# Rotary embedding of half the head on one core: three whole tiles loaded first, then stores and the last load in another order

## The chip, the cores and the metric

One core of a Trainium2 chip runs the kernel. The metric is the device time of one execution in microseconds (us). The kernel before takes 161.53 us in the median of 8 runs (161.33 to 161.8).

## The reference

`x` is (16, 512, 16, 64) in float32: batch, position, head, dimension. `cos` and `sin` are (512, 32), of which only the first 16 columns are used. Of each head's 64 numbers the first 32 are rotated as two quarters of 16, and the last 32 are copied:

```
x1, x2 = x[..., :32], x[..., 32:]
rotated_first  = x1[..., :16] * cos[..., :16] - x1[..., 16:] * sin[..., :16]
rotated_second = x1[..., :16] * sin[..., :16] + x1[..., 16:] * cos[..., :16]
out = concatenate([rotated_first, rotated_second, x2], axis=-1)
```

So 33.55 MB are read and 33.55 MB are written, with four elementwise passes over half of the data in between.

## The kernel before

**Tiles.** The 8192 rows of `x` (batch times position, each of 16 x 64 numbers) are cut into T = 4 tiles. A tile has 128 partitions with K = 16 neighbouring rows each, 64 KB to a partition, 8.39 MB in all. `ring` (L45) is one buffer in SBUF with NS = 3 slots; tile t lies in slot t % 3, so tile 3 takes the slot of tile 0 and can be loaded only when tile 0 has been stored. The rotation works in place in the slot, and the store reads from the slot, which carries the copied half along.

**Transfers.** `load` (L54, recorded as L55) and `store` (L57, recorded as L58) move rows lo to hi of each partition of one tile. Both are issued by SyncE (SP), one after the other in the order of the program; an instruction of SP that waits holds up all behind it. Only tile 2's store is issued by GpSimd (POOL), on a queue of its own (q0; SP's is q1). Both queues are worked off by the same 16 DMA engines.

**Tables.** `cos` and `sin` are loaded by POOL (L63, L64), spread over the partitions by a shuffle and copies on VectorE (DVE, L73 to L86), and end up in `table`.

**Rotation.** `rotate(t, lo, hi)` (L90) is four DVE instructions over rows lo to hi of a tile: two multiplications (L96 into `b_t` in PSUM, L97 in place), a subtraction (L98) and an addition (L101). A tile is rotated in two pieces of 8 rows (KC = 8), tile 2 in pieces of 8, 5 and 3 rows (KM = 13).

**Order.** SP issues load(0), load(1), the first half of load(2); then, when tile 0 is rotated, store(0), the second half of load(2) and load(3), which waits for store(0) to land; then store(1), then store(3). DVE rotates the tiles 0, 1, 2, 3 in turn. store(1) would be free to go when tile 1 is rotated; a dependency written by hand (L118) makes it wait for the end of the 5-row piece of tile 2 (`near`, L114). store(2), on POOL, goes when tile 2 is rotated.

Of the kernel before, what the change touches and what calls it, by code (L numbers as in the profile page):

```python
# [1 line left out]

# [4 lines left out]


@with_exitstack
def kernel(  # L10
    ctx: ExitStack,
    tc: tile.TileContext,
    x: bass.AP,
    cos: bass.AP,
    sin: bass.AP,
    out: bass.AP,
):
    nc = tc.nc
    fp32 = mybir.dt.float32
    P = 128  # L20
    B, S, H, D = x.shape
    Q = D // 4
    HF = D // 2

    K = 16
    T = B * S // (P * K)
    PB = S // K
    REP = P // PB  # L30
    R = H * D
    NS = 3
    KC = K // 2
    KM = 13

    xf = x.rearrange("b s h d -> (b s h d)").rearrange("(t p f) -> t p f", t=T, p=P)
    of = out.rearrange("b s h d -> (b s h d)").rearrange("(t p f) -> t p f", t=T, p=P)
    cosf = cos.rearrange("(p k) j -> p (k j)", k=K)
    sinf = sin.rearrange("(p k) j -> p (k j)", k=K)

    const_pool = ctx.enter_context(tc.tile_pool(name="const", bufs=1))
    b_pool = ctx.enter_context(tc.tile_pool(name="bp", bufs=1, space=bass.MemoryType.PSUM))


    ring = const_pool.tile([P, NS, K, H, D], fp32)  # L45
    stage = const_pool.tile([P, 2, K, HF], fp32)
    spun = const_pool.tile([P, 2 * K, Q], fp32)
    packed = const_pool.tile([PB, 2 * K, Q], fp32)
    table = const_pool.tile([P, 2, K, 2, Q], fp32)

    def rows(t, lo, hi):
        return ring[:, t % NS, lo:hi].rearrange("p k h d -> p (k h d)")

    def load(t, lo=0, hi=K):  # L54
        return nc.sync.dma_start(out=rows(t, lo, hi), in_=xf[t, :, lo * R : hi * R])  # L55

    def store(t, lo=0, hi=K, queue=nc.sync):  # L57
        return queue.dma_start(out=of[t, :, lo * R : hi * R], in_=rows(t, lo, hi))  # L58


    nc.vector.memset(stage[:, :, :, 0:Q], 0.0)  # L61
    spread = stage.rearrange("(j b) t k i -> j b t (k i)", b=REP)
    nc.gpsimd.dma_start(out=spread[:, 0, 0], in_=cosf)  # L63
    nc.gpsimd.dma_start(out=spread[:, 0, 1], in_=sinf)  # L64
    load(0)
    load(1)
    load(2, 0, KC)

    PQ = PB // REP
    nc.vector.stream_shuffle(  # L73
        out=spun[:],
        in_=stage.rearrange("p t k j -> p (t k) j")[:, :, 0:Q],
        mask=[j % PQ * REP for j in range(PB)],
    )
    for q in reversed(range(REP)):
        n = PQ * (q + 1)
        nc.vector.tensor_copy(out=packed[0:n], in_=spun[q * PB : q * PB + n])  # L80

    for r in range(REP):
        nc.vector.tensor_copy(  # L83
            out=table[r * PB : (r + 1) * PB].rearrange("p t k c j -> p (t k) c j"),
            in_=packed.unsqueeze(2).to_broadcast((PB, 2 * K, 2, Q)),
        )  # L86
    C = table[:, 0].rearrange("p k c j -> p k (c j)")
    Sn = table[:, 1].rearrange("p k c j -> p k (c j)")

    def rotate(t, lo, hi):  # L90
        x1 = ring[:, t % NS, lo:hi, :, 0:HF]
        c = C[:, lo:hi].unsqueeze(2).to_broadcast((P, hi - lo, H, HF))
        s = Sn[:, lo:hi].unsqueeze(2).to_broadcast((P, hi - lo, H, HF))
        b_full = b_pool.tile([P, KC, H, HF], fp32, name="b_t")
        b_t = b_full[:, 0 : hi - lo]
        nc.vector.tensor_mul(out=b_t, in0=x1, in1=s)  # L96
        nc.vector.tensor_mul(out=x1, in0=x1, in1=c)  # L97
        nc.vector.tensor_sub(  # L98
            out=x1[:, :, :, 0:Q], in0=x1[:, :, :, 0:Q], in1=b_t[:, :, :, Q:HF]
        )  # L100
        return nc.vector.tensor_add(  # L101
            out=x1[:, :, :, Q:HF], in0=x1[:, :, :, Q:HF], in1=b_t[:, :, :, 0:Q]
        )

    rotate(0, 0, KC)
    rotate(0, KC, K)
    store(0)
    load(2, KC, K)
    load(3)
    rotate(1, 0, KC)  # L110
    rotate(1, KC, K)
    behind_loads = store(1)
    rotate(2, 0, KC)
    near = rotate(2, KC, KM)  # L114
    rotate(2, KM, K)
    store(2, queue=nc.gpsimd)

    tc.add_manual_dep(  # L118
        behind_loads.ins,
        near.ins.name,  # L120
        mybir.DependencyInfo(mybir.DependencyClass.Sync, mybir.DependencyReason.DATA),
        reason="the store follows the loads at the DMA engines",
    )
    rotate(3, 0, KC)
    rotate(3, KC, K)
    store(3)


# [1 line left out]
_INS = ['x', 'cos', 'sin']  # L130
_OUTS = [((16, 512, 16, 64), 'float32')]


# [23 lines left out]
```

## Time and profile before

| what | value |
|---|---|
| median of 8 runs | 161.53 us (161.33 to 161.8) |
| the profiled execution | 161.36 us, span 159.4 us |
| DVE busy | 112.9 us (71%), 47 instructions |
| POOL busy | 1.9 us |
| the 16 DMA engines | 67.24 MB, 98% of the span (85.6% for SP's queue, 12.4% for POOL's) |
| one 8-row rotation | 13.44 us; 4.43, 4.42, 2.29 and 2.28 us for its four instructions, the last two overlapping slightly |
| DVE idle ahead of the first rotation | 14.3 us for `sin`, then 1.8 us for tile 0 |

How to read it: the span is the time from the first to the last instruction of the profiled execution; the device time is 2.0 us more. A transfer is seen at three points: its issue, an instruction on SP or POOL; the packets that the 16 engines move for it; and its landing, when all 16 engines have reported the end. The list of DMA issues gives the median time from issue to landing; asked for a stretch that holds one issue alone, it gives the time of that one. What stands in the queue ahead of a transfer is part of that time. Where both queues have work, packets of POOL's and of SP's take turns in this trace.

### The profile page before, as it was taken

How to read it: one execution, taken by the hardware profiler on the slowest of the kernel's cores; microseconds unless marked ns; L12 is line 12 of the kernel's file. 1: busy time of each engine (PE TensorE's matmuls, PEld its weight loads, DVE VectorE, ACT ScalarE, POOL GpSimd, SP SyncE). 2: the span in 40 equal slices, each digit the busy share in tenths (PEclk: the TensorE clock that was granted, in tenths of full speed). 3: DMA queues.
4: the chain of work that ended last, by engine and by line, in shares of the span. 5: the costliest groups of instructions: out<-in, count | busy, mean ns of one | idle time of the engine just before them, and what ended most of it. 6: DMA issues, size and time to landing. Idle time of an engine off the chain costs nothing.

```text
span 159.4 us, 115 instructions
## 1 busy us (share of the span) xinstructions
DVE 112.9 (71%) x47; POOL 1.9 (1%) x7
## 2 busy tenths in 40 slices
DVE  1000959999999999999999999999999990000000
POOL 3000000000000000000000000010000000000000
DMA  7969979799699699699996996996996996998966
GB/s 263 543 263 543 444 345 526 345 444 526 280 493 543 263 526 526 263 395 461 461 526 280 510 526 263 526 526 263 526 526 263 526 493 296 526 428 362 526 263 263
DMA packets 1360, 67.24 MB, mean 422 GB/s; under 512 B 176, under 2 KB 176, under 8 KB 208
## 3 DMA queue, kind: packets, MB, share of 16 engines
q1 hardware_dynamic: 1152, 58.72, 85.6%
q0 software_dynamic: 208, 8.52, 12.4%
HBM read 33.69 MB, written 33.55 MB: 422 GB/s over the span
## 4 chain that ended last, share of the span: by engine, by line
DVE 62%; DMA 14%; issue 5%; DVEq 1%
DVE b_t L96 22%; DVE ring L97 22%; DMA ring<-in_x_dram 14%; DVE ring L101 10%; DVE ring L98 7%; DVEq L152 1%; DVEq L96 0%
## 5 line engine op out<-in xcount | busy, mean ns | idle before, releaser
L96 DVE TENSOR_TENSOR b_t<-ring,table 128x4096 f32<-128x4096 f32 (+2 forms) x9 | 35.6, 3959 | 2.1 <-DMA ring<-in_x_dram 1.8
L97 DVE TENSOR_TENSOR ring<-ring,table 128x4096 f32<-128x4096 f32 (+2 forms) x9 | 35.6, 3951 | 0.3
L98 DVE TENSOR_TENSOR ring<-ring,b_t 128x2048 f32<-128x2048 f32 (+2 forms) x9 | 18.5, 2050 | 0.3
L101 DVE TENSOR_TENSOR ring<-ring,b_t 128x2048 f32<-128x2048 f32 (+2 forms) x9 | 18.4, 2043 | 0.0
L73 DVE LOAD_MASK_SELECT spun<-stage x1 | 0.0, 14 | 14.3 <-DMA stage<-in_sin_dram 14.3
L83 DVE COPY table<-packed 32x1024 f32<-32x1024 f32 x4 | 2.7, 683 | 0.1
L58 POOL DMA_DIRECT2D out_dram<-ring x1 | 0.6, 559 | 101.6 <-DVE ring L101 101.6
L80 DVE COPY packed<-spun 32x512 f32<-32x512 f32 (+3 forms) x4 | 1.7, 416 | 0.1
L61 DVE MEMSET stage<- 128x512 f32 x1 | 0.5, 485 | 0.9 <-PEq L141 0.9
L73 DVE STREAM_SHUFFLE spun<-stage 128x512 f32<-128x512 f32 x1 | 0.7, 723 | 0.0
L63 POOL DMA_DIRECT2D stage<-in_cos_dram x1 | 0.6, 642 | 1.3 <-DVE stage L61 1.3
L64 POOL DMA_DIRECT2D stage<-in_sin_dram x1 | 0.5, 532 | 0.0
L141 POOL MEMSET const-bfloat16-1.0<- 128x1 bf16 x1 | 0.1, 101 | 0.0
L141 POOL MEMSET const-float32-0.0<- 128x1 f32 x1 | 0.1, 98 | 0.2 <-issue 0.2
L141 POOL MEMSET const-float32-1.0<- 128x1 f32 x1 | 0.1, 98 | 0.0
L141 POOL MEMSET const-uint8-127<- 128x1 uint8 x1 | 0.1, 98 | 0.0
## 6 DMA issues: line engine op xcount, KB each, us to landing
ring<-in_x_dram SPq DMA_DIRECT2D x2, 4096.0 KB, 40.7
stage<-in_cos_dram POOLq DMA_DIRECT2D x1, 64.0 KB, 8.9
stage<-in_sin_dram POOLq DMA_DIRECT2D x1, 64.0 KB, 13.2
ring<-in_x_dram SPq DMA_DIRECT2D x3, 29.0
out_dram<-ring SPq DMA_DIRECT2D x3, 27.4
out_dram<-ring POOLq DMA_DIRECT2D x1, 39.5
```

The lines of the kernel that those rows point to most:

```text
L58: return queue.dma_start(out=of[t, :, lo * R : hi * R], in_=rows(t, lo, hi))
L61: nc.vector.memset(stage[:, :, :, 0:Q], 0.0)
L63: nc.gpsimd.dma_start(out=spread[:, 0, 0], in_=cosf)
L64: nc.gpsimd.dma_start(out=spread[:, 0, 1], in_=sinf)
L73: nc.vector.stream_shuffle(out=spun[:], in_=stage.rearrange("p t k j -> p (t k) j")[:, :, 0:Q], mask=[j % PQ * REP for j in range(PB)],)
L80: nc.vector.tensor_copy(out=packed[0:n], in_=spun[q * PB : q * PB + n])
L83: nc.vector.tensor_copy(out=table[r * PB : (r + 1) * PB].rearrange("p t k c j -> p (t k) c j"), in_=packed.unsqueeze(2).to_broadcast((PB, ...
L96: nc.vector.tensor_mul(out=b_t, in0=x1, in1=s)
L97: nc.vector.tensor_mul(out=x1, in0=x1, in1=c)
L98: nc.vector.tensor_sub(out=x1[:, :, :, 0:Q], in0=x1[:, :, :, 0:Q], in1=b_t[:, :, :, Q:HF])
L101: return nc.vector.tensor_add(out=x1[:, :, :, Q:HF], in0=x1[:, :, :, Q:HF], in1=b_t[:, :, :, 0:Q])
L152: with _tile.TileContext(nc) as tc:
```

## The change

The loads in front are three whole tiles. store(0), ready when tile 0 is rotated, waits by hand for the third instruction (the subtraction) of the first piece of tile 1. Tile 1 is rotated in pieces of 7, 7 and 2 rows (KA = 7, KB = 14), tile 2 in two of 8. The first half of store(1) goes when its 14 rows are rotated; then tile 3 is loaded in two halves, ordered behind it on SP without a wait of their own for it. The second half of store(1) waits for the first multiplication of tile 3's first piece, and store(2), still on POOL, for the second one. store(3) is as before. `rotate` now returns its first three instructions.

```
-    load(2, 0, KC)
+    load(2)
...
     rotate(0, 0, KC)
     rotate(0, KC, K)
-    store(0)
-    load(2, KC, K)
-    load(3)
-    rotate(1, 0, KC)
-    rotate(1, KC, K)
-    behind_loads = store(1)
+    head = store(0)
+    behind(head, rotate(1, 0, KA)[2])
+    rotate(1, KA, KB)
+    rotate(1, KB, K)
+
+
+    part = store(1, 0, KC)
+    for lo, hi in ((0, KC), (KC, K)):
+        follow(load(3, lo, hi), part)
     rotate(2, 0, KC)
-    near = rotate(2, KC, KM)
-    rotate(2, KM, K)
-    store(2, queue=nc.gpsimd)
-
-    tc.add_manual_dep(
-        behind_loads.ins,
-        near.ins.name,
-        mybir.DependencyInfo(mybir.DependencyClass.Sync, mybir.DependencyReason.DATA),
-        reason="the store follows the loads at the DMA engines",
-    )
-    rotate(3, 0, KC)
+    rotate(2, KC, K)
+    marks = rotate(3, 0, KC)
+    behind(store(1, KC, K), marks[0])
+    behind(store(2, queue=nc.gpsimd), marks[1])
     rotate(3, KC, K)
     store(3)
```

`behind` is the same dependency by hand as before (a wait on a semaphore), and `follow` one that only fixes the order of issue on an engine:

```
+    def behind(transfer, point, kind=mybir.DependencyClass.Sync):
+        tc.add_manual_dep(
+            transfer.ins,
+            point.ins.name,
+            mybir.DependencyInfo(kind, mybir.DependencyReason.DATA),
+            reason="issue the transfer near the end of the one in front of it",
+        )
+
+    def follow(transfer, other):
+        behind(transfer, other, mybir.DependencyClass.NoSync)
```

More of the change, by code (lines that the diff above doesn't have):

```diff
@@ L33 @@
     KC = K // 2
-    KM = 13
+    KA, KB = 7, 14
     xf = x.rearrange("b s h d -> (b s h d)").rearrange("(t p f) -> t p f", t=T, p=P)
@@ L95, in rotate @@
         b_t = b_full[:, 0 : hi - lo]
-        nc.vector.tensor_mul(out=b_t, in0=x1, in1=s)
-        nc.vector.tensor_mul(out=x1, in0=x1, in1=c)
-        nc.vector.tensor_sub(
+        first = nc.vector.tensor_mul(out=b_t, in0=x1, in1=s)
+        second = nc.vector.tensor_mul(out=x1, in0=x1, in1=c)
+        third = nc.vector.tensor_sub(
             out=x1[:, :, :, 0:Q], in0=x1[:, :, :, 0:Q], in1=b_t[:, :, :, Q:HF]
         )
-        return nc.vector.tensor_add(
+        nc.vector.tensor_add(
             out=x1[:, :, :, Q:HF], in0=x1[:, :, :, Q:HF], in1=b_t[:, :, :, 0:Q]
         )
+        return first, second, third
+    def behind(transfer, point, kind=mybir.DependencyClass.Sync):
[7 more added lines that the diff above has]
+        behind(transfer, other, mybir.DependencyClass.NoSync)
     rotate(0, 0, KC)
     rotate(0, KC, K)
-    store(0)
-    load(2, KC, K)
-    load(3)
-    rotate(1, 0, KC)
-    rotate(1, KC, K)
-    behind_loads = store(1)
-    rotate(2, 0, KC)
-    near = rotate(2, KC, KM)
-    rotate(2, KM, K)
-    store(2, queue=nc.gpsimd)
-    tc.add_manual_dep(
-        behind_loads.ins,
-        near.ins.name,
-        mybir.DependencyInfo(mybir.DependencyClass.Sync, mybir.DependencyReason.DATA),
-        reason="the store follows the loads at the DMA engines",
-    )
-    rotate(3, 0, KC)
+    head = store(0)
[5 more added lines that the diff above has]
+        follow(load(3, lo, hi), part)
+    rotate(2, 0, KC)
+    rotate(2, KC, K)
+    marks = rotate(3, 0, KC)
+    behind(store(1, KC, K), marks[0])
+    behind(store(2, queue=nc.gpsimd), marks[1])
     rotate(3, KC, K)
```

## The prediction

> **What bounds the kernel now.** I read the summary first, then the chain of work that ended last, then the issues of DMAs one at a time, then the order of instructions around the edits.
>
> ```profile
> DVE 112.9 (71%) x47; POOL 1.9 (1%) x7
> ...
> DMA packets 1360, 67.24 MB, mean 422 GB/s; under 512 B 176, under 2 KB 176, under 8 KB 208
> ...
> q1 hardware_dynamic: 1152, 58.72, 85.6%
> q0 software_dynamic: 208, 8.52, 12.4%
> ...
> DVE 62%; DMA 14%; issue 5%; DVEq 1%
> ```
>
> The chain names DVE, because it starts at the last instruction and goes back through the issue of store(3), which waits for DVE. But the two queues keep the 16 DMA engines at 98% of the span. Which of the two decides is read from the time from issue to landing, here of single issues, in stretches that hold one each: store(0) issued at 49.82, load(3) at 71.6, store(1) at 98.80, store(2) at 104.52 and store(3) at 131.1.
>
> ```profile
> out_dram<-ring SPq DMA_DIRECT2D x1, 21.8
> ...
> ring<-in_x_dram SPq DMA_DIRECT2D x1, 29.0
> ...
> out_dram<-ring SPq DMA_DIRECT2D x1, 33.2
> ...
> out_dram<-ring POOLq DMA_DIRECT2D x1, 39.5
> ...
> out_dram<-ring SPq DMA_DIRECT2D x1, 27.4
> ```
>
> Issue plus time gives the landings: store(0) 71.6, load(3) 100.6, store(1) 132.0, store(2) 144.0, store(3) 158.5. By the same sum load(0) lands at 0.74 + 22.1 = 22.8, load(1) at 1.2 + 41.0 = 42.2, the halves of tile 2 at 1.6 + 50.3 = 51.9 and 50.2 + 31.1 = 81.3. A tile behind another takes 19.3 to 19.4 (load(1) after load(0), load(3) after the second half of tile 2). Three stores lie between 100.6 and 158.5: 57.9 = 3 x 19.3. So nothing idles there, and store(3) needs 27.4 instead of 19.3 only because 8 us of older stores stand in front of it. DVE could end several us later and change nothing. The stages by windows say the same (columns: length, DVE and POOL busy, clock, DMA share, GB/s):
>
> ```profile
> 51.30:99.90 48.60, 48.18 (x17) 0.00 (x0) 1.00 1.00 430
> 70.50:99.50 29.00, 28.72 (x12) 0.00 (x0) 1.00 1.00 434
> 99.50:157.50 58.00, 31.34 (x12) 0.56 (x1) 1.00 1.00 434
> ```
>
> The transfers decide, and they already run back to back at 434 GB/s. What is lost after the start is small: store(0) takes 71.6 - 51.9 = 19.7 from the landing in front, **0.4 more** than a tile, where the engines go over from a store to a load. The change moves the same bytes, so it can win at most about this 0.4 and otherwise only lose, by letting the engines run dry.
>
> **The change, step by step.** The end is a sum of landings; each edit is asked whether the next transfer is there in time.
>
> *How early must one be issued?* store(1) was issued at 98.80, 1.8 ahead of the landing of load(3) at 100.6, and the three stores after it lost nothing: a lead of 1.8 is enough. From the other side: load(0), with nothing ahead, lands 22.1 after its issue, 2.8 more than a tile (some of it the table's packets). So the lead needed lies between 0 and 2.8; I take 1.8, the row of a store behind a load, as the nearest.
>
> *Three whole tiles first.* The second half of tile 2 comes forward: load(2) lands at 51.9 + 9.7 = 61.6. DVE reads it only at about 77, so nobody waits for it.
>
> *store(0) held back.* Nothing else on SP is ready, so its wait delays no one. Tile 0's rotation ends at 49.83 as before. The 5-row and the 8-row piece take 90.16 to 98.81 = 8.65 and 76.72 to 90.16 = 13.44, so 1.60 per row and 0.65 on top; 7 rows take 11.84. The subtraction starts after two multiplications of about 3.92 and lasts 2.29 - 0.27 = 2.02: it ends at 59.7. Issue at 59.72 against load(2) at 61.6 is a lead of 1.8, the proven one. Cost 0; at the other bound 1.0.
>
> ```profile
> 97.30 1.48 DVE L101 TENSOR_TENSOR ring<-ring,b_t 128x1280 f32<-128x1280 f32 x1
> 98.80 0.34 SPq L58 DMA_DIRECT2D out_dram<-ring  x1
> ...
> 104.26 4.43 DVE L96 TENSOR_TENSOR b_t<-ring,table 128x4096 f32<-128x4096 f32 x1
> 104.52 0.56 POOL L58 DMA_DIRECT2D out_dram<-ring  x1 [101.65 <-DVE ring L101]
> ```
>
> These rows give the price of a wait by hand: the addition ends at 98.78 and SP issues at 98.80; POOL needs 0.26 after its release.
>
> *First half of store(1), then load(3).* The first two pieces of tile 1 end at 49.83 + 2 x 11.84 = 73.5, and the half store queues on SP then; store(0) is on the engines until 61.6 + 19.3 = 80.9. Load(3), behind it on SP, waits for that landing and is issued at about 81, while the half store covers the engines until 80.9 + 9.7 = 90.6. So the wait of SP is hidden by 9 us of store; without this half in between it would cost up to 2.8. The 0.4 for going from store to load is paid here instead of at 71: half store lands 91.0, the halves of load(3) 100.6 and **110.3**.
>
> *Rotations.* The number of DVE instructions is unchanged (nine pieces), so is the sum: tile 1 gains 0.65 for a third piece, tile 2 loses it. Tile 3's first piece starts at 104.26 as before; its half is there since 100.6. The second piece starts at 117.7, against 110.3.
>
> *Second half of store(1).* It waits for the first multiplication: 104.26 + 4.43 = 108.7. Lead 110.3 - 108.7 = 1.6, **0.2 short** of the proven one; only store(3), not due until 131.1, is behind it on SP. Cost 0 if less lead is needed, 1.2 if 2.8 is. I take 0.1, near the row of 1.8, because an early engine among the 16 waits longer than the late one that sets the landing.
>
> *store(2).* The second multiplication ends at 104.26 + 4.47 + 4.42 = 113.15, POOL issues at 113.4. Before, its first packets appear in a stretch that begins 4.9 after the issue at 104.52, with SP's packets in front; 113.4 + 4.9 = 118.3, while the half store lasts until 110.3 + 9.7 = 120. Hidden. The queue of POOL then works alone until store(3) arrives at 131.1, when about 8 us of store(2) are left, the same cover as before.
>
> *Cut transfers.* Two halves cost 9.7 + 9.7 against 19.3 for a whole: at most 0.1. There are four halves instead of two: 0.05 taken.
>
> *Sum.* 110.3 + 0.1 + 2.5 x 19.3 + 0.05 = 158.7 for the last landing, against 158.5: **+0.15 to 0.2**. On the profiled execution of 161.36 that is 161.5; its time lies 0.17 below the median of the runs, and on the median of 161.53 it is **161.7**.
>
> A rule that speaks against the change: the Trainium skill, "DMA: Bandwidth & Descriptors", section "Rules for kernel authors", wants a DMA issued early, so that its fixed cost is overlapped, and the section "Anatomy of one DMA" puts that cost at about 2.0 us; a lead of 1.8 and one of 1.6 would then lose 0.2 and 0.4, and my estimate by that page is 162.1. The row at 98.80, with 1.8 and no loss, speaks for the lower end, and the sum above uses only the row.
>
> **Rivals.**
>
> *Leads too short (slower), 0.25.* store(0) and the second half of store(1) come too late, and the engines run dry twice. For it: load(0)'s 2.8 with empty queues. Against it: the row at 98.80. It decides from a needed lead of 1.9 (0.1 + 0.3 = 0.4 together). At 2.8 it costs 1.0 + 1.2 = 2.2 and gives 163.7; half way, at 2.3, 0.5 + 0.7 = 1.2 and 162.7.
>
> *The turn gets cheaper (faster), 0.12.* The 0.4 at the turn from store to load falls away, as the stream turns between transfers of half a tile, and the leads suffice: 161.1. Against it: the number of such turns stays at one, and if load(3) landed 0.4 earlier, at 109.9, the lead of the second half would shrink to 1.2.
>
> *POOL's queue alone is slower, 0.05.* From 120 to 131 only store(2) is left for the engines. The trace has no such stretch. If it ran at half of the rate there, 11 us would move 5.5 us of work: 167.
>
> *The change doesn't do what it says, 0.02.* If load(3) came ahead of the half store on SP, the engines would be empty from 80.9 until load(3) starts: up to 2.8, 164.4.
>
> **Chances and range.** Forecast, within 0.2% (0.3 us, about what a measurement of this kernel can tell): 0.56. Faster by more: 0.12. Slower by more: 0.25 + 0.05 + 0.02 = 0.32. Range: down to 161.1 for the cheaper turn, up to 162.8, past the half-way case of the short leads; beyond that lie the full 2.8 and the last two rivals, some 0.17 in all.
>
> **What would show it.** Right: load(2) lands near 61.6, store(0) issues near 59.7 and lands at 80.9 to 81.3, load(3) near 110.3, store(3) near 158.7, DMA share at 1.00 in windows around 61 and 110. Short leads: the landing of store(0) minus that of load(2) well over 19.7, or the last 2.5 tiles taking over 48.4. A slow POOL queue: GB/s under 430 between 120 and 131. A cheaper turn: under 48.7 from the landing of load(2) to that of load(3). I would be wrong at the root if DVE ended last, that is, if store(3) were issued later than 138, when store(2) runs out.

## The result, and the profile after

The changed kernel takes 162.30 us in the median of 11 runs (162.03 to 163.24), the kernel before 161.52 (31 runs). The ratio is **1.0058**, 95% interval 1.0046 to 1.0069: slower by 0.8 us. The profiled execution took 162.25 us with a span of 160.2, against 161.36 and 159.4.

The summary of the changed kernel's page, the lines that answer to those of the prediction:

```profile
DVE 112.9 (70%) x47; POOL 1.9 (1%) x7
...
DMA packets 1504, 67.24 MB, mean 420 GB/s; under 512 B 192, under 2 KB 192, under 8 KB 224
...
DVE 62%; DMA 14%; issue 4%; DVEq 1%
```

VectorE does the same work in the same time, and the bytes are the same. There are more packets, because four transfers are halves instead of two, and the mean rate falls from 422 to 420 GB/s. So the time went at the DMA engines, and the landings say where. Single issues of the changed kernel with their times to landing: store(0), issued at 59.82, the first half of store(1) at 73.6, its second half at 108.80, store(2) at 113.53, store(3) at 131.2:

```profile
out_dram<-ring SPq DMA_DIRECT2D x1, 21.2
...
out_dram<-ring SPq DMA_DIRECT2D x1, 4096.0 KB, 17.7
...
out_dram<-ring SPq DMA_DIRECT2D x1, 4096.0 KB, 16.6
...
out_dram<-ring POOLq DMA_DIRECT2D x1, 31.2
...
out_dram<-ring SPq DMA_DIRECT2D x1, 27.9
```

The halves of load(3), issued at 81.0 and 81.4, needed 20.1 and 29.4; load(2), issued at 1.6, needed 60.0.

| landing, us | predicted | measured |
|---|---|---|
| load(2) | 61.6 | 61.6 |
| store(0) | 80.9 | 81.0 |
| first half of store(1) | 91.0 | 91.3 |
| load(3), first half | 100.6 | 101.1 |
| load(3), second half | 110.3 | 110.8 |
| store(3) | 158.7 | 159.1 |

Up to 81.0 all is as predicted, and from 110.8 to the end 48.3 pass, against 48.4 predicted. In between, where the engines go over from a store to loads, 0.4 more is lost than predicted (29.8 instead of 29.4). The rest is mostly at the end: the span ends 1.1 after the last landing instead of 0.9.

**A measure of the loss.** A turn, below, is the place where the engines go over from loads to a store, or from a store to loads. In a window, GB/s over DMA share is the speed of the packets while they run. Both count whole packets, so the edges of a short window can push the share above or below 1, but not their quotient. The undisturbed value is 434. Share x length x (1 - speed/434) is the time lost to slow packets; idle gaps between packets are not in it and show in the landings. The windows (length, DVE and POOL busy, clock, DMA share, GB/s) of the kernel before at its turn from load to store (46 to 56), its turn from store to load (66 to 76), and late in the stores:

```profile
46.00:56.00 10.00, 9.93 (x4) 0.00 (x0) 1.00 1.03 446
66.00:76.00 10.00, 9.93 (x4) 0.00 (x0) 1.00 0.87 364
...
146.00:156.00 10.00, 0.00 (x0) 0.00 (x0) 1.00 1.00 433
```

and of the changed kernel at its turns from load to store (56 to 66, 105 to 115) and from store to load (85 to 95):

```profile
56.00:66.00 10.00, 9.90 (x5) 0.00 (x0) 1.00 1.12 485
85.00:95.00 10.00, 9.93 (x4) 0.00 (x0) 1.00 1.02 410
105.00:115.00 10.00, 9.93 (x3) 0.56 (x1) 1.00 1.03 446
```

446/1.03 and 485/1.12 are 433: at the turns from load to store no packets are slow, before and after. At the turn from store to load the speed is 364/0.87 = 418 before, a loss of 0.3, and 410/1.02 = 402 after, a loss of **0.75**. The engines do not run dry there, since the packets of the trace follow each other without a gap; they run slower. The slow ones are the last store packet of the engines and some of the first loads: the last 32 KB packet took 1.5 to 2.3 us instead of 1.21; before, the last 64 KB packet took 2.4 to 3.2 instead of 2.42.

### The profile page after: what moved, and what is told of

Read it like the earlier page. It is cut to its first block, busy times and chain, and to the rows that moved or that the text cites. A ratio compares the mean times of both kernels' runs of the same rounds, so it can differ in the third digit from the quotient of the medians.

```text
span 160.2 us, 117 instructions
## 1 busy us (share of the span) xinstructions
DVE 112.9 (70%) x47; POOL 1.9 (1%) x7
## 4 chain that ended last, share of the span: by engine, by line
DVE 62%; DMA 14%; issue 4%; DVEq 1%
DVE b_t L96 22%; DVE ring L97 22%; DMA ring<-in_x_dram 14%; DVE ring L101 10%; DVE ring L98 8%; DVEq L162 1%; DVEq L96 0%
## 6 DMA issues: line engine op xcount, KB each, us to landing
out_dram<-ring POOLq DMA_DIRECT2D x1, 31.2
```

## The experiments

Ratios are to the kernel before on the same chip, from 5 rounds each; the losses come from windows of 10 us by the measure above, in one profiled execution, and are good to about 0.1 (share and rate are rounded). Each kernel turns twice from load to store; one number is that of the first turn, two are those of both.

| kernel | ratio (95%) | load to store | store to load |
|---|---|---|---|
| before | 1 | 0, 0 | 0.3 |
| changed | 1.0058 (1.0046 to 1.0069) | 0, 0 | 0.75 |
| b_s0_halves | 1.0073 (1.0060 to 1.0086) | 0.85 | 0.1 |
| b_s0_tail | 1.0024 (1.0015 to 1.0033) | 0 | 0.5 |
| b_l2_16k | 1.0057 (1.0043 to 1.0071) | 1.0 | 0.05 |
| a_s1_parts | 1.1352 (1.1336 to 1.1367) | - | - |
| a_load_near | 1.0056 (1.0041 to 1.0071) | 0, 0 | 0.85 |
| a_s0_early | 1.0060 (1.0046 to 1.0073) | 1.1, 0 | 0 |
| b_s1_early | 1.0063 (1.0049 to 1.0078) | 0, 1.2 | 0.45 |
| b_load_near | 1.0013 (1.0005 to 1.0022) | 0 | 0.7 |
| b_s0_halves_near | 1.0032 (1.0020 to 1.0044) | 0 | 0.7 |
| b_load_9us | 1.0000 (0.9991 to 1.0009) | 0 | 0.4 |
| a_s1_whole | 1.0054 (1.0040 to 1.0069) | 0, 0.1 | 0.8 |
| b_s0_2_14 | 1.0018 (1.0009 to 1.0027) | 0.2 | 0.3 |

Names with b_ are edits of the kernel before, with a_ of the changed one. The first theory (A) was that the halved store, whose packets are 32 KB, covers less of the start of the loads behind it.

**b_s0_halves**

```
-    store(0)
+    store(0, 0, KC)
+    store(0, KC, K)
```

> The kernel before with store(0) issued as two halves of 8 rows, so that the packets in front of the turn from store to load are 32 KB instead of 64 KB; what follows the turn is unchanged. The turn is measured as the time from the landing of the last load of the first batch to the landing of load(3), less 2.5 tiles of 19.3 us: 0.5 us in the kernel before, 1.0 in the changed one. Theory A (a small store packet in front of the turn covers less of the start of the loads): turn 0.8 to 1.1, time up by 0.3 to 0.6 us, ratio 1.002 to 1.004. Theory B (the size of the load packets behind the turn, or how they are cut, sets the price): turn 0.4 to 0.6, ratio 0.9995 to 1.001. Theory C (the waits by hand, POOL's queue or the end of the stream make the changed kernel slower, the turn only by chance): as B.

Slower by more than A asks, and for another reason. Its windows, at the turn from load to store and at the one from store to load:

```profile
46.00:56.00 10.00, 9.93 (x4) 0.00 (x0) 1.00 1.02 406
68.00:78.00 10.00, 9.93 (x4) 0.00 (x0) 1.00 1.02 439
```

The loss moved to the turn from **load to store** (406/1.02 = 398), and the other turn became all but free (430). Without a wait of its own, the first half of store(0) was issued at 36.45, when its 8 rows were rotated, and stood in the queue for some 13 us ahead of its turn.

**b_s0_tail**

```
-    store(0)
+    store(0, 0, 14)
+    store(0, 14, K)
```

> The kernel before with store(0) cut into 14 and 2 rows, so that the last packets in front of the turn are 8 KB. A: the price of the turn rises beyond that of 32 KB, to 1.0 to 1.5 us, ratio 1.003 to 1.007. B and C: turn 0.4 to 0.6, ratio at most 1.001.

Its window at the turn from store to load:

```profile
66.00:76.00 10.00, 9.93 (x4) 0.00 (x0) 1.00 0.99 406
```

Between the theories: slower by 0.24%, with a loss of 0.5 at the turn (406/0.99 = 410, of which some 0.06 is the greater length of 8 KB packets for their bytes). A, by which 8 KB should cost more than 32 KB, does not fit as a rule of size.

**b_l2_16k**

```
-    load(2, 0, KC)
+    load(2, 0, 12)
...
-    load(2, KC, K)
+    load(2, 12, K)
```

> The kernel before with 12 rows of tile 2 in the first batch and 4 behind the turn: the first load packets behind the turn are 16 KB instead of 32 KB, the store in front is unchanged (64 KB). The first batch is 2.75 tiles, and the turn is measured from its last landing less 2.25 tiles. A: turn 0.4 to 0.6, ratio 0.999 to 1.001. B: turn 0.7 to 1.0, ratio 1.002 to 1.004. C: ratio 0.999 to 1.001.

The ratio is B's, but not the place. The windows at the turn from load to store and from store to load:

```profile
51.00:61.00 10.00, 9.93 (x3) 0.00 (x0) 1.00 0.96 372
72.00:82.00 10.00, 9.90 (x5) 0.00 (x0) 1.00 0.97 419
```

372/0.96 = 388 is a loss of 1.0 at the turn from load to store, where store(0), issued at 50.03, had stood in the queue for about 6 us. The turn to the 16 KB loads is free (419/0.97 = 432), if behind a turn that was paid, so the agreement with B is by chance. B cannot explain the change in any case, since the loads behind the turn are of 32 KB packets in both kernels.

**a_s1_parts**

```
-    part = store(1, 0, KC)
+    def store_part(t, lo, hi):
+        return nc.sync.dma_start(out=of[t, lo:hi, :], in_=ring[lo:hi, t % NS].rearrange("p k h d -> p (k h d)"))
+
+    part = store_part(1, 0, 64)
...
-    behind(store(1, KC, K), marks[0])
+    behind(store_part(1, 64, 128), marks[0])
```

> The changed kernel with tile 1's store halved by partitions (0 to 63, then 64 to 127, all 16 rows) instead of by rows: same bytes in each half, but packets of 64 KB in front of the turn; waits, loads and queues unchanged, the first half goes at 77.4 instead of 73.5, still ahead of the end of store(0). A: turn back to 0.4 to 0.6, 0.4 to 0.6 us faster than the changed kernel, ratio to before 1.000 to 1.003. B and C: turn 0.9 to 1.1, ratio 1.004 to 1.007.

It says nothing on A: a store of 64 partitions ran at half the rate. The window of its first half:

```profile
80.00:100.40 20.40, 20.23 (x7) 0.00 (x0) 1.00 0.99 207
```

The engines are busy for the whole of it, but a 64 KB packet takes 5.1 us instead of 2.42.

After these runs the theories were about how long a transfer of the other direction has been queued: D (it slows the turn in either direction), E (only the first such turn of a run is paid), F (going from store to load costs, whatever the lead).

**a_load_near**

```
-    for lo, hi in ((0, KC), (KC, K)):
-        follow(load(3, lo, hi), part)
-    rotate(2, 0, KC)
+    thirds = [load(3, lo, hi) for lo, hi in ((0, KC), (KC, K))]
+    for transfer in thirds:
+        follow(transfer, part)
+    behind(thirds[0], rotate(2, 0, KC)[2])
```

> The changed kernel with one wait more: the first half of load(3) waits for the subtraction of tile 2's first piece (end near 88.7 us), about 1.2 us ahead of the end of the half store in front, instead of being queued from 81.0. Theory D (a transfer of the other direction that is queued well ahead of the turn slows the last packets in front of it; one issued about 1 us ahead does not): packets in front of the turn back to 1.2 us, 0.6 to 0.8 us faster than the changed kernel, ratio to before 0.998 to 1.001. Theory E (only the first early-queued turn of a run is paid): the same here. Theory F (going from store to load costs this, whatever the lead): unchanged, 1.004 to 1.007, or slower by a gap.

Issued at 88.90, just ahead of the turn, and nothing won: 1.0056. The window at the turn:

```profile
85.00:95.00 10.00, 9.93 (x4) 0.00 (x0) 1.00 1.05 419
```

419/1.05 = 399. D's gain did not come, but half of what D said did. Short windows that hold only the last store packets (from 88.50) and only the first load packets (from 90.00) show it, first in the changed kernel, then in a_load_near:

```profile
88.50:89.50 1.00, 1.00 (x2) 0.00 (x0) 1.00 1.87 524
90.00:91.20 1.20, 1.17 (x2) 0.00 (x0) 1.00 1.10 437
...
88.50:89.50 1.00, 1.00 (x2) 0.00 (x0) 1.00 1.24 524
90.00:91.20 1.20, 1.17 (x2) 0.00 (x0) 1.00 1.59 437
```

With the load queued early the last store packets are slow (524/1.87 = 280) and the first loads less so (437/1.10 = 397). With the load issued late the store packets are normal (423) and the first loads slow (437/1.59 = 275). So the time of issue decided which packets paid, and not how much.

**a_s0_early**

```
     head = store(0)
-    behind(head, rotate(1, 0, KA)[2])
+    rotate(1, 0, KA)
```

> The changed kernel without the wait of store(0): it is queued at 49.9, some 11 us ahead of the turn from load to store near 61, instead of at 59.8. D: that turn now costs 0.8 to 1.0 us too, ratio to before 1.009 to 1.012. E: the first turn is paid and the turn from store to load is free, so about as the changed kernel, 1.004 to 1.007. F: no change at 61, 1.004 to 1.007, the turn from store to load still paid.

Windows at the turns load to store (61), store to load (91), load to store (110):

```profile
54.00:64.00 10.00, 9.93 (x4) 0.00 (x0) 1.00 0.87 328
87.00:97.00 10.00, 9.93 (x4) 0.00 (x0) 1.00 1.00 433
105.00:115.00 10.00, 9.93 (x3) 0.56 (x1) 1.00 0.97 419
```

328/0.87 = 377: store(0), now issued at 49.93, costs 1.1 at its turn, and the turn from store to load costs nothing. The sum hardly moves: 1.0060. E describes this.

**b_s1_early**: the call of `tc.add_manual_dep` for `behind_loads` is left out.

> The kernel before without the wait of store(1), which is then queued at about 76.7, some 23 us ahead of the turn from load to store near 99.8. D: 0.8 to 1.0 us slower, ratio 1.005 to 1.007, the loss in the packets around 97 to 100. E: the turn near 70 is early-queued too and comes first (0.3 us paid as before), so this one is free: 0.999 to 1.001. F: no change, 0.999 to 1.001.

Windows at the turns load to store (51), store to load (71), load to store (100):

```profile
46.00:56.00 10.00, 9.93 (x4) 0.00 (x0) 1.00 1.05 452
66.00:76.00 10.00, 9.93 (x4) 0.00 (x0) 1.00 0.89 367
93.00:103.00 10.00, 9.83 (x7) 0.00 (x0) 1.00 0.86 321
```

The early store costs 1.2 (321/0.86 = 373), although the turn near 71 was paid too. E falls as it was put. What holds in all four kernels with an early store (b_s0_halves, b_l2_16k, a_s0_early, b_s1_early): it costs 0.85 to 1.2. Where a turn from store to load follows (three of them), that one is nearly free.

**b_load_near**: the second half of load(2) waits for a multiplication of tile 1, which is cut 6, 8, 2; store(1) waits for the subtraction of its piece instead of the addition.

```
+    rotate(1, 0, 6)
+    point = rotate(1, 6, 14)[1]
+    rotate(1, 14, K)
...
+    tc.add_manual_dep(
+        rest.ins,
+        point.ins.name,
...
-    near = rotate(2, KC, KM)
+    near = rotate(2, KC, KM)[2]
```

> The kernel before with the second half of load(2) issued at about 69.0 (wait for the second multiplication in a piece of 8 rows of tile 1, now cut 6, 8, 2) instead of at 50.2, so 1.1 to 1.5 us ahead of the end of store(0); the wait of store(1) is moved to the subtraction of the same 5-row piece (98.0 us, since the further piece of tile 1 adds 0.65 on VectorE). D and E: the 0.3 us in the packets at 68 go, 0.2 to 0.5 us faster, ratio 0.997 to 0.999. F: unchanged or slower by a small gap, 1.000 to 1.003.

Its window at the turn:

```profile
66.00:76.00 10.00, 9.90 (x5) 0.00 (x0) 1.00 0.90 360
```

Slower by 0.13%, with 0.7 lost at the turn (360/0.90 = 400): a load issued late, at 69.17, is no help and probably a little worse. Here too the last store packets took their normal 2.42 us and the first loads were slow (1.2 to 2.2 us instead of 1.21). D's gain falls, F stands. That left the size of the price: why 0.3 before and 0.75 after? G blames how long the load had been queued.

**b_s0_halves_near**: store(0) in halves, the first with a wait for the end of tile 0's rotation.

```
...
-    store(0)
...
+    head = store(0, 0, KC)
...
+    store(0, KC, K)
```

> The kernel before with store(0) in two halves again, both issued at 49.8 as the whole was, so that the turn from load to store stays unpaid and only the packets in front of the turn from store to load change, from 64 KB to 32 KB. Theory A (the small store packet in front of the turn): loss at the turn near 70 about 0.8 us instead of 0.3, ratio 1.003 to 1.005. Theory G (the time for which load(3) had been queued: 9 us in the changed kernel, 20 before): 0.3 to 0.45 us, ratio 1.000 to 1.0015.

As A said: 1.0032, and the turn from store to load costs 0.7.

```profile
46.00:56.00 10.00, 9.93 (x4) 0.00 (x0) 1.00 0.99 426
66.00:76.00 10.00, 9.93 (x4) 0.00 (x0) 1.00 0.93 374
```

374/0.93 = 402, the speed that the changed kernel has at its turn; the first turn is free (430).

**b_load_9us**: the second half of load(2) waits for the subtraction of tile 1's first piece.

```
+    point = rotate(1, 0, KC)[0]
...
+    tc.add_manual_dep(
+        rest.ins,
+        point.ins.name,
```

> The kernel before with the second half of load(2) issued at 61.0 instead of 50.2, 9 to 10 us ahead of the end of store(0) as load(3) is in the changed kernel; store packets of 64 KB. A: loss at the turn 0.3 to 0.4 us, ratio 0.999 to 1.001. G: 0.6 to 0.9 us, ratio 1.002 to 1.004.

```profile
66.00:76.00 10.00, 9.93 (x4) 0.00 (x0) 1.00 0.91 377
```

1.0000 (0.9991 to 1.0009), and 377/0.91 = 414 is a loss of 0.4. G falls.

**a_s1_whole**

```
-    part = store(1, 0, KC)
+    part = store(1)
...
-    marks = rotate(3, 0, KC)
-    behind(store(1, KC, K), marks[0])
-    behind(store(2, queue=nc.gpsimd), marks[1])
-    rotate(3, KC, K)
+    marks = rotate(3, 0, KA)
+    behind(store(2), marks[1])
+    rotate(3, KA, KB)
+    rotate(3, KB, K)
```

> The changed kernel with the whole of store(1) in front of load(3), so packets of 64 KB in front of the turn, and load(3) queued 19 us ahead of it; load(3) then lands 10 us later, tile 3 is rotated in 7, 7 and 2 rows, and store(2) goes on SP behind the second multiplication of the first of them, about 1.5 us ahead of the end of the loads. A and G both: loss at the turn near 100 us 0.3 to 0.45 instead of 0.8, ratio 1.000 to 1.003. If the price belongs to the changed order as such: 0.7 to 1.0 us lost, 1.004 to 1.007.

Both theories missed: with 64 KB packets in front of the turn it still costs 0.8.

```profile
95.00:105.00 10.00, 9.32 (x4) 0.00 (x0) 1.00 0.85 334
```

334/0.85 = 393. Further short gaps, some 0.3 in all by the packets of the trace, came with store(2) and store(3), issued at 118.97 and 138.6, only 1.8 and 1.4 ahead of the landings in front of them (120.8 and 140.1). So in the changed order the small packet is not needed for the high price. What a_s1_whole shares with b_s0_halves_near is a second store transfer between the two turns; the last run tests that (I).

**b_s0_2_14**: as b_s0_halves_near, with 2 instead of KC rows in the first part.

> The kernel before with store(0) cut into 2 and 14 rows, both issued at 49.8: two store transfers in front of the turn from store to load as in the changed kernel, but the packets next to the turn are 56 KB, nearly those of the whole store. Theory A (a small packet next to the turn): loss at the turn 0.3 to 0.45 us, ratio at most 1.0012. Theory I (two store transfers in front of the turn, whatever their packets): 0.6 to 0.9 us, ratio 1.002 to 1.004.

```profile
66.00:76.00 10.00, 9.93 (x4) 0.00 (x0) 1.00 1.01 426
```

At the turn A's answer, 0.3 (426/1.01 = 422): a second store transfer by itself does not raise the price. The ratio of 1.0018 is above A's bound, though. Of the 0.29 us some 0.16 lie behind the last landing, where the span ends 1.05 later instead of 0.88, as in the other kernels with one transfer more on SP. The profiled execution also lost a little in its packets (some 0.15 around 31 to 39, and 0.2 around the turn from load to store, of the table), for which there is no theory.

## Why the prediction was right and wrong

**Right.** The DMA engines bound both kernels, and VectorE never ended last: store(3) was issued at 131.2, while store(2) landed only at 144.7 (113.53 + 31.2). The landings up to store(0) held within 0.1. The leads were enough: store(0) landed 19.4 behind load(2), where well over 19.7 would have shown a late issue, and the last 2.5 tiles took 48.3, not over 48.4. POOL's queue alone fed the engines without loss, though not from 120 as predicted. The second half of store(1) landed at 125.4 (108.80 + 16.6), because the packets of both queues took turns from about 118 on. In a window with data of store(2) alone:

```profile
123.00:131.00 8.00, 7.97 (x3) 0.00 (x0) 1.00 0.91 393
```

393/0.91 = 432, the normal speed.

**Wrong.** The forecast of no change (0.56) missed, and of the slower cases (0.32 together) the named ones did not happen: no lead was too short. That the time still lies in the range is luck, for its upper end had been set for short leads. The step that failed is "the 0.4 for going from store to load is paid here instead of at 71". It took the price of a turn as a constant that moves with it. By landings the turn cost 0.45 before (51.9 to 100.6, less 2.5 x 19.3) and 0.95 after (61.6 to 110.8); that 0.5, with 0.1 spread over the landings before and behind the turn and 0.2 between the last landing and the end of the span, is the difference of the two spans (0.8). The sum also ended at the last landing and took the end of the span as unchanged, although SP issues one transfer more: from the last landing to the end of the span pass 0.88 in the five kernels of this case in which SP issues 8 transfers, and 1.04 to 1.06 in the nine in which it issues 9. What takes these 0.16 to 0.18 was not followed up. The rival of a cheaper turn looked at the same term with the other sign: "as the stream turns between transfers of half a tile" was its reason for a gain, and the halved store in front made the turn dearer.

**What the runs show of the cause.** Shown: the price of the turn from store to load is not fixed. The difference does not come from how long the load had been queued (9 us ahead instead of 20: ratio 1.0000; 1 to 2 us ahead of the end of the store packets: none better), nor from the load's packets, which are of 32 KB in both kernels. Issuing the load late moves the loss from the last store packets to the first load packets and saves nothing. Halving store(0) in the kernel before, with the order kept, raises the price from 0.3 to 0.7 and the time by 0.32%, about half of what the change costs. Some 0.1% of that (0.16 us) belongs to the transfer more on SP and not to the turn: b_s0_2_14, with the same number of transfers, was slower by 0.18% at a price of 0.3.

**Open.** Small store packets are not the whole cause: in the changed order a whole store of 64 KB packets paid 0.8 as well, and 8 KB packets only 0.5. What in that order keeps the price at 0.75 to 0.85 in all three kernels that have it (more store traffic since the last turn, the place of the data, or something else) was not separated. Nor is it known why a turn that was paid at load to store makes the next one free.

**The rule that was weighed.** The prediction weighed the rule of an early issue (the Trainium skill, "DMA: Bandwidth & Descriptors", "Rules for kernel authors") and estimated from it a loss of 0.2 and 0.4 for the late stores. It took the 2.0 us for that from the section "Anatomy of one DMA", which gives it for DMAs issued by GpSimd; these two stores were issued by SP. No run agrees with such a loss: leads of 1.8 and 2.0 lost nothing, and taking the wait away from store(0) or store(1) made the packets at that turn lose 1.1 and 1.2 us. For a store behind loads, at engines that are busy throughout, the measurement decides against an earlier issue.

None of the kernels was faster than the kernel before.

## What to carry to other kernels

When the DMA engines are busy throughout, count the turns between loading and storing, and price each by its own window: GB/s over DMA share shows packets that run slower while the share still reads full. Issue a store about 2 us ahead of the landing of the loads in front of it. Leads of 1.8 to 2.1 lost nothing in the two kernels; leads of 6 us and more cost 0.85 to 1.2 us at that turn, after which the next turn to loads was nearly free. Do not halve the store in front of a turn to loads without measuring it, and count each transfer more: here one more on SP went with 0.16 us behind the last landing.

## What the runs showed of the hardware

A store that names only 64 of the 128 partitions ran at half the rate: 5.1 us for a 64 KB packet instead of 2.42, 207 GB/s instead of 434, with the engines reading as fully busy. A store queued 6 us or more ahead of the turn slowed the last load packets (in b_l2_16k those of all engines: a 48 KB one took 2.5 to 3.1 us instead of 1.8). At a turn from store to load, a load queued 9 us ahead left the last 32 KB store packets at 1.5 to 2.3 us instead of 1.21; issued 1 to 1.5 us ahead of their end, it left them at 1.21 to 1.28, and its own first packets took 1.45 to 2.4. Packets of 64, 48, 32 and 16 KB otherwise ran at one rate (2.42, 1.82, 1.21 and 0.61 us), so the packets of a cut transfer were as fast as those of a whole one. One transfer more on SP went with a longer end of the span, 1.04 to 1.06 us behind the last landing instead of 0.88.
